# A pooled subtraction streamed through six tile buffers: the last tile subtracted and stored in two halves, the second left to the framework

## The chip, the core and the metric

The kernel runs on one core of one Trainium2 chip. The metric is the device time of one execution in microseconds (us). The profiler also gives the span, from the first to the last instruction, which in these runs is 1.7 to 2.2 us shorter than the time. The record calls an execution slow when it is over 1.5% above the fastest of its kernel.

## The reference

The input is 8 x 4096 x 2112 in fp32. Every four consecutive rows are averaged, and the average is taken from each of the four.

```python
x_r = x.reshape(B, S // stride, stride, D)      # B, S, D = 8, 4096, 2112; stride = 4
pooled = x_r.mean(axis=2)
upsampled = np.repeat(pooled, stride, axis=1)
return (x - upsampled).astype(np.float32)
```

## The kernel before

A group of four rows is one contiguous run of 33,792 bytes. A tile is 128 groups, one per partition, 4224 KB in all; there are n = 64 tiles and six buffers ("slots"). The sync engine (SP) issues the loads, VectorE (DVE) makes three additions and one subtraction per tile, in place (the sums of successive tiles alternate between two buffers, `s_sb` and `s_ps`), and ScalarE (ACT) issues the stores. The section `tile_critical` is synchronised by hand: a load waits for the store that empties its slot, a store for the count of finished subtractions. After it, POOL waits for the last six stores.

```python
def reduce_tile(b, parity):
    rows = slots[b].rearrange("p (f d) -> p f d", f=STRIDE)
    s = s_ps if parity else s_sb
    nc.vector.wait_ge(load_sems[b], 16).then_inc(load_sems[b], -16)
    # ... three additions: s = the sum of the four rows, chained by step_sem
    adds = STRIDE - 1
    nc.vector.wait_ge(step_sem, adds).then_inc(step_sem, -adds)
    nc.vector.scalar_tensor_tensor(
        out=rows, in0=s[:, None, :].to_broadcast([P, STRIDE, D]),
        scalar=-1.0 / STRIDE, in1=rows,
        op0=mybir.AluOpType.mult, op1=mybir.AluOpType.add,
    ).then_inc(done_sem)

with tc.tile_critical():
    for k in range(n):                     # loads, on SP's queue
        # ... b, lap = slot and round of tile k
        load = nc.sync.dma_start(out=slots[b][:], in_=xg[k * P:(k + 1) * P])
        if lap:
            load._wait_ge(store_sems[b], 16 * lap)
        load.then_inc(load_sems[b], 16)
    # ... VectorE: reduce_tile for each tile, in a loop over laps, the rest unrolled
    for k in range(n):                     # stores, on ACT's queue
        # ... b = slot of tile k
        store = nc.scalar.dma_start(out=og[k * P:(k + 1) * P], in_=slots[b][:])
        store._wait_ge(done_sem, k + 1)
        store.then_inc(store_sems[b], 16)
for k in range(n - SLOTS, n):
    total = nc.gpsimd.to_reg(16 * (k // SLOTS + 1))
    tc.keep_in_program_order(nc.gpsimd.wait_ge(store_sems[k % SLOTS], total))
```

## Time and profile before

| | before |
|---|---|
| time, median of the first 3 runs (range) | 1285.41 us (1285.28 to 1285.58) |
| span of the profiled run | 1283.7 us |
| VectorE busy | 1026.4 us, 80% |
| moved | 553.66 MB, mean 431 GB/s |
| last subtraction ends / last store issued / lands | 1268.5 / 1268.6 / 1282.8 us |

The lines behind this table stand in the prediction.

### The profile page before, as it was taken

Reading aid. Unit: us, or ns where it says so; the run is one execution under the profiler, and the core shown is the slowest. Engines: PE = TensorE matmul, PEld = TensorE weight load, DVE = VectorE, ACT = ScalarE, POOL = GpSimd, SP = SyncE. Lnnn points to the kernel's source line nnn. Section 1 sums busy time; section 2 is a strip of 40 time slices with the busy share of each in tenths; the row PEclk is TensorE's granted clock in tenths of the full one; section 3 lists DMA queues with packets and bytes.
Section 4 is the critical chain, followed back from the end, with each engine's and each line's share of the span. In section 5 each row is a group of like instructions: output and inputs, shape, how many; then the busy total and the mean of one; then the engine's idle time right before and its main releaser. Section 6 shows DMA issues by size and latency. Waiting matters only on the chain. (4 is left out here: it accounts for less than half of the span.)

```text
span 1283.7 us, 591 instructions
## 1 busy us (share of the span) xinstructions
DVE 1026.4 (80%) x256; POOL 0.2 (0%) x4
## 2 busy tenths in 40 slices
DVE  5998788787787877878778787787887878878775
POOL 0000000000000000000000000000000000000000
DMA  9999999999999999999999999999999999999999
GB/s 404 421 438 433 426 438 430 431 437 438 430 430 438 431 434 433 438 430 430 438 431 436 431 438 430 430 438 433 435 430 438 430 431 437 438 430 430 438 430 396
DMA packets 18433, 553.66 MB, mean 431 GB/s; under 512 B 2048, under 2 KB 2048, under 8 KB 2048
## 3 DMA queue, kind: packets, MB, share of 16 engines
q1 hardware_dynamic: 9216, 276.83, 50.1%
q10 hardware_dynamic: 9216, 276.83, 50.0%
q14 instruction: 1, 0.01, 0.0%
HBM read 276.82 MB, written 276.82 MB: 431 GB/s over the span
## 5 line engine op out<-in xcount | busy, mean ns | idle before, releaser
L67 DVE SCALAR_TENSOR_TENSOR slot<-s_sb,slot 128x8448 f32<-128x8448 f32 x32 | 286.7, 8958 | 4.7 <-DVEq L66 0.2
L67 DVE SCALAR_TENSOR_TENSOR slot<-s_ps,slot 128x8448 f32<-128x8448 f32 x32 | 286.6, 8957 | 4.7
L59 DVE TENSOR_TENSOR s_sb<-slot 128x2112 f32<-128x2112 f32 x32 | 75.4, 2357 | 120.1 <-DVEq L58 120.1
L59 DVE TENSOR_TENSOR s_ps<-slot 128x2112 f32<-128x2112 f32 x32 | 75.7, 2366 | 108.2 <-DVEq L58 108.2
L62 DVE TENSOR_TENSOR s_ps<-s_ps,slot 128x2112 f32<-128x2112 f32 x64 | 151.4, 2366 | 2.2
L62 DVE TENSOR_TENSOR s_sb<-s_sb,slot 128x2112 f32<-128x2112 f32 x64 | 150.9, 2358 | 2.2
L116 POOL MEMSET const-bfloat16-1.0<- 128x1 bf16 x1 | 0.1, 102 | 0.0
L116 POOL MEMSET const-uint8-127<- 128x1 uint8 x1 | 0.1, 101 | 0.0
L116 POOL MEMSET const-float32-0.0<- 128x1 f32 x1 | 0.1, 99 | 0.2 <-issue 0.2
L116 POOL MEMSET const-float32-1.0<- 128x1 f32 x1 | 0.1, 99 | 0.0
## 6 DMA issues: line engine op xcount, KB each, us to landing
slot<-in_x_dram SPq DMA_DIRECT2D x64, 4224.0 KB, 59.7
out_dram<-slot ACTq DMA_DIRECT2D x64, 4224.0 KB, 43.6
```

What stands on the lines that cost most here:

```text
L59: add = nc.vector.tensor_add(out=s[:], in0=rows[:, 0, :], in1=rows[:, 1, :])
L62: add = nc.vector.tensor_add(out=s[:], in0=s[:], in1=rows[:, f, :])
L67: nc.vector.scalar_tensor_tensor(out=rows, in0=s[:, None, :].to_broadcast([P, STRIDE, D]), scalar=-1.0 / STRIDE, in1=rows, op0=mybir.AluOp ...
L116: nc = _bacc.Bacc("TRN2", target_bir_lowering=False, num_devices=1)
```

## The change

Its intent: start storing the last tile when half of it is subtracted, so that less is left to store after VectorE's last instruction. The second half store stands after the hand-synchronised section, where the framework finds its waits and its semaphore. "By rows" means the rows of a group: the first half is rows 0 and 1 of each group, the first 4224 columns of every partition.

```diff
-    def reduce_tile(b, parity):
+    def reduce_tile(b, parity, cuts=(0, STRIDE)):
...
-        nc.vector.scalar_tensor_tensor(
-            out=rows,
-            in0=s[:, None, :].to_broadcast([P, STRIDE, D]),
...
-        ).then_inc(done_sem)
+        for lo, hi in zip(cuts, cuts[1:]):
+            nc.vector.scalar_tensor_tensor(
+                out=rows[:, lo:hi, :],
+                in0=s[:, None, :].to_broadcast([P, hi - lo, D]),
...
+            ).then_inc(done_sem)
...
+        half = STRIDE // 2
         for b in range(rest):
-            reduce_tile(b, b % 2)
+            reduce_tile(b, b % 2, (0, STRIDE) if b < rest - 1 else (0, half, STRIDE))
...
-            store = nc.scalar.dma_start(out=og[k * P:(k + 1) * P], in_=slots[b][:])
+            cols = W if k < n - 1 else half * D
+            store = nc.scalar.dma_start(
+                out=og[k * P:(k + 1) * P, :cols], in_=slots[b][:, :cols]
+            )
             store._wait_ge(done_sem, k + 1)
             store.then_inc(store_sems[b], 16)
+
+    nc.scalar.dma_start(out=og[G - P:, half * D:], in_=slots[rest - 1][:, half * D:])
```

More of the change, by code (lines that the diff above doesn't have):

```diff
@@ L66, in reduce_tile @@
         nc.vector.wait_ge(step_sem, adds).then_inc(step_sem, -adds)
-        nc.vector.scalar_tensor_tensor(
-            out=rows,
-            in0=s[:, None, :].to_broadcast([P, STRIDE, D]),
-            scalar=-1.0 / STRIDE,
-            in1=rows,
-            op0=mybir.AluOpType.mult,
-            op1=mybir.AluOpType.add,
-        ).then_inc(done_sem)
+        for lo, hi in zip(cuts, cuts[1:]):
+            nc.vector.scalar_tensor_tensor(
+                out=rows[:, lo:hi, :],
+                in0=s[:, None, :].to_broadcast([P, hi - lo, D]),
+                scalar=-1.0 / STRIDE,
+                in1=rows[:, lo:hi, :],
+                op0=mybir.AluOpType.mult,
+                op1=mybir.AluOpType.add,
+            ).then_inc(done_sem)
     assert SLOTS % 2 == 0
```

## The prediction

> **What bounds the kernel now.** I read the first page of the profile from the top: the busy shares, the slices, the transfer queues, and only then the chain that ended last.
>
> ```profile
> DVE 1026.4 (80%) x256; POOL 0.2 (0%) x4
> ...
> DMA  9999999999999999999999999999999999999999
> GB/s 404 421 438 433 426 438 430 431 437 438 430 430 438 431 434 433 438 430 430 438 431 436 431 438 430 430 438 433 435 430 438 430 431 437 438 430 430 438 430 396
> ...
> q1 hardware_dynamic: 9216, 276.83, 50.1%
> q10 hardware_dynamic: 9216, 276.83, 50.0%
> ```
>
> The transfer engines stand at 9 in all forty slices and the load and store queues together fill 100.1% of their time. VectorE (DVE) is at 80%. 64 loads and 64 stores of 4224 KB each are 553.66 MB, and in the middle slices they move at 430 to 438 GB/s. So the kernel is bound by transfers, and the change saves no byte of them. It can only act at the end, and the chain view speaks of VectorE there:
>
> ```profile
> 2 pieces in order of time: start us, us, what
> 1259.48 0.08 issue
> 1259.56 8.96 DVE slot L67
> ```
>
> This is the last tile's subtraction, ending at 1268.5, followed by 15.2 us of the 1283.7 us span in which the view names nothing. That gap is what the change aims at: the last store (4.3 MB) cannot start before the subtraction ends. The question is whether the transfer engines were idle while they waited for it. Two views answer. The first is by stretches (columns: stretch, length, VectorE busy, POOL busy, clock, transfer share, GB/s), from the landing of the last load (the last tile's first add starts at 1252.25) to the issue of the last store, and from there on:
>
> ```profile
> 1252.25:1268.60 16.35, 16.06 (x4) 0.00 (x0) 1.00 1.00 430
> 1268.60:1281.20 12.60, 0.00 (x0) 0.00 (x0) 1.00 0.99 429
> ```
>
> In the first stretch no load is left, the last store is not issued yet, and still the engines are at 1.00 and 430 GB/s. What they move are stores already queued. The second view is the store line, asked in three windows of 20 us, each of which holds the issue of one store, the third last to the last:
>
> ```profile
> L94 ACTq DMA_DIRECT2D out_dram<-slot x1: 338/338/338, 1228.6 to 1228.6; - x1
> DMA to landing us min/median/max: 34.2/34.2/34.2
> ...
> L94 ACTq DMA_DIRECT2D out_dram<-slot x1: 339/339/339, 1248.5 to 1248.5; - x1
> DMA to landing us min/median/max: 24.2/24.2/24.2
> ...
> L94 ACTq DMA_DIRECT2D out_dram<-slot x1: 338/338/338, 1268.6 to 1268.6; - x1
> DMA to landing us min/median/max: 14.2/14.2/14.2
> ```
>
> Issue plus time to landing gives the landings: 1228.6 + 34.2 = 1262.8, 1248.5 + 24.2 = 1272.7, 1268.6 + 14.2 = 1282.8. They lie 9.9 and 10.1 us apart, and one store at 430 to 435 GB/s takes 4.325 MB / 0.43 to 0.435 = 9.9 to 10.1 us. The three stores therefore ran back to back: **the last one was issued 4.1 us before its predecessor landed and stood in line behind it.** VectorE's end isn't what sets the last landing; the queue is. After 1282.8 there remain 0.9 us of semaphores and barriers to 1283.7.
>
> [...]
>
> **The change, part by part.**
>
> (a) The last subtraction in two halves of 4224 columns. [...] First half done at 1259.56 + 4.56 = 1264.1, second at 1268.7.
>
> (b) First half store, 2.163 MB, issued at about 1264.2 in place of 1268.6, 4.4 us earlier. It queues behind the store that lands at 1272.7, as the whole one did. Gain on the time: none. Its share of the line is 5.0 us, so it should land near 1277.7.
>
> (c) Second half store, outside the hand-synchronised section. In the built program it waits until SP has collected the ends of SP, ScalarE's and VectorE's parts of that section, and carries a semaphore of the framework's. Before, SP's collecting step, which stands in the program already, came at 1269.1 with nothing depending on it:
>
> ```profile
> L78 DVEq DRAIN  x1: 8970/8970/8970, 1259.6 to 1259.6; - x1
> L78 ACTq DRAIN  x1: 153/153/153, 1268.9 to 1268.9; - x1
> L78 SPq NOP  x1: 13/13/13, 1269.1 to 1269.1; - x1
> ```
>
> Here VectorE's drain ends at 1268.5, ScalarE drains after issuing the whole store, and SP follows 0.6 us after VectorE. After the change ScalarE has drained long before and VectorE sets the moment: I expect SP at 1268.8 to 1269.1 and the second half issued at 1269.0 to 1269.3, up to 0.7 us **later** than the whole store before. It stands in line behind the first half until about 1277.7. How long does a store take from issue to landing with nothing before it? The first load, 4224 KB with no other in front of it, took 12.4 us (the shortest load in the trace), so about 2.4 us beyond its data. The second half thus needs to be issued only by some 1277.7 - 2.4 = 1275.3; it is there 6 us early. The delay is hidden whole.
>
> (d) Added work of the transfer engines. The bytes are the same; there is one more transfer with its 16 semaphore packets, and 128 rows in two pieces. The pieces per engine are 8 before and 16 after. In the steady state two transfers take 19.97 us (the additions of the even tiles start 1212.31 and 1252.25, four transfers in 39.94), that is 9.985 us each [...]
>
> (e) The end. Before, POOL waits for the store semaphores (its branch comes at 1282.8) and the barrier takes 0.9 us. After, POOL is released at 1277.7 and waits in the barrier; SP waits for the framework's semaphore and joins last. One waiter in place of another: I put it at 0 +- 0.15 us.
>
> Sum: 0 (a, hidden) + 0 (b) + 0 (c) + 0.05 (d) + 0.0 (e). From 1285.41 this gives 1285.46, **1285.5 us**, with the span near 1283.8.
>
> **The rivals.**
>
> The overlap works. If the transfer engines were idle until the last store came, 4.4 us earlier issue of half of it would save up to 4.4 us: 1281.0. For it speaks the chain view, which ends on the subtraction; against it the share of 1.00 and 430 GB/s while the subtraction runs, and the landings 10 us apart. Even this would be 0.3% and inside the 2%.
>
> The framework's store waits for more than the section's ends, such as the landing of the first half. Then it would start at 1277.7 plus about half a microsecond, with some 2.4 us of latency exposed: 1288 us. Against it: its waits in the built program are on the engines' sequencers[...].
>
> The smaller pieces or a shorter tail help. If the engines finish unevenly, half-sized rows could even out the end, or a completion that depends on the last row's size could come up to 0.6 us (half of the 1.25 us in which one engine moves a 33,792-byte row) sooner: 1284.8. Nothing in the trace demands it; the same unevenness may cost as much. The instruction fetch, one packet of 8 KB on the instruction queue, may also fall at another place; a landing shift of a few tenths either way is possible.
>
> **Range and chances.** The three runs before lie within 0.3 us, so the machine's scatter is small; what is uncertain is the tail: 0.15 us in the barrier, up to 0.6 us from the ends of the engines, and a change of session. I take 1284.6 to 1286.2. Faster or slower by 2% would be 25.7 us, more than the whole time after VectorE's last instruction (15.2 us), so neither half store can gain it, and a loss of that size would need a serialisation that no wait in the program makes. Faster 0.005, same 0.985, slower 0.01.
>
> **What would show each step right or wrong.** In the profile after: two subtractions of 128x4224, about 4.56 us each; the first half store issued near 1264.2 and landing near 1277.7, so over 13 us for 5 us of data; the second issued near 1269.2 and landing near 1282.8, over 13 us too; transfer share about 1.0 through to 1281; SP ending a wait near 1282.8 in POOL's place. I am wrong on (b) if the first half lands before 1275, on (c) if the second half is issued after 1271 or the share drops between the halves, on (d) and (e) if the last landing or the barrier moves by over 0.3 us.

The sum came to 0.05 us, all of it from (d), so 1285.41 + 0.05 = 1285.46; that 0.05 is the estimate. It was measured only later (0.050, in the experiment with 256 transfers). For the packets of (d), the pages show 18,433 before and 18,577 after: 144 more, 16 semaphore packets and 128 pieces. The 4.56 us of a half subtraction can be estimated from the trace as well: a straight line through the 2357 ns of an addition of 2112 columns and the 8957 ns of the subtraction of 8448 gives 4557 ns for 4224. And that the waits at the exit of the section don't include landings shows in the kernel before: SP's collecting step came at 1269.1, 13.7 us before the last store landed at 1282.8.

## The result, and the profile after

| | before | after |
|---|---|---|
| time, median of 6 runs (range) | 1285.35 us (1285.09 to 1285.58) | 1285.19 us (1285.04 to 1287.81) |
| ratio of the fast runs | | 1.0002, 95% interval 0.9989 to 1.0015 |
| span of the profiled run | 1283.7 us | 1283.4 us |

The same time. A ratio here is the mean of one kernel's fast runs over the mean of the other's from the same rounds, so it isn't quite the ratio of the medians. One of the six runs after took 1287.81 us and pulls the mean up; without it they lie between 1285.04 and 1285.25. The medians differ by 0.16 us, less than the range of the runs before. Such single runs, 2 to 6 us above the rest, also came with the kernel before (1287.24 us in a later batch) and with an experiment (1291.09 us); what causes them was not looked into.

The chain of waits of the changed kernel (columns: start, length, what) ends with VectorE's drain at the exit of the section, which waits for the second half of the subtraction. It stops at 1268.9, 14.5 us before the end of the span at 1283.4 (15.2 us in the kernel before).

```profile
3 pieces in order of time: start us, us, what
1259.79 0.08 issue
1259.87 4.56 DVE slot L69
1264.43 4.46 DVEq L80
```

The two halves of the subtraction (shortest, median and longest in ns, first and last start):

```profile
L69 DVE SCALAR_TENSOR_TENSOR slot<-s_ps,slot x2: 4545/4551/4557, 1259.9 to 1264.3; 128x4224 f32<-128x4224 f32 x2
```

The same stretches as before, from the landing of the last load to the end of the line (columns as in the prediction), show the transfer engines just as full.

```profile
1252.25:1268.60 16.35, 15.83 (x5) 0.00 (x0) 1.00 1.00 430
1268.60:1281.20 12.60, 0.29 (x1) 0.00 (x0) 1.00 0.99 426
```

The lines of the second last store, of the first half and of the second half (when the transfer was issued, and how long it took to land):

```profile
L98 ACTq DMA_DIRECT2D out_dram<-slot x1: 338/338/338, 1248.9 to 1248.9; - x1
DMA to landing us min/median/max: 23.6/23.6/23.6
...
L98 ACTq DMA_DIRECT2D out_dram<-slot x1: 338/338/338, 1264.5 to 1264.5; - x1
DMA to landing us min/median/max: 13.0/13.0/13.0
...
L104 ACTq DMA_DIRECT2D out_dram<-slot x1: 338/338/338, 1269.1 to 1269.1; - x1
DMA to landing us min/median/max: 13.4/13.4/13.4
```

They land at 1272.5, 1277.5 and 1282.5: back to back again, 5.0 us for each half. The first half was issued 4.1 us earlier than the whole store had been and took 13.0 us for 5.0 us of data. The time it gained at VectorE it spent in line.

The exit of the hand-synchronised section, and the end:

```profile
L80 ACTq DRAIN  x1: 152/152/152, 1264.8 to 1264.8; - x1
L80 SPq NOP  x1: 13/13/13, 1269.0 to 1269.0; - x1
...
L135 POOLq COMPARE_BRANCH  x1: 33/33/33, 1277.5 to 1277.5; - x1
```

ScalarE left the section at 1264.8, VectorE at 1268.9, SP collected both at 1269.0 and the second half went out at 1269.1. POOL came free when the first half landed, at 1277.5 in place of 1282.8; SP waited for the second, and the end came 0.9 us after the last landing, as before.

### The profile page after: what moved, and what is told of

It is laid out like the page before. It is cut to its first block, busy times and chain, and to the rows that moved or that the text cites. A ratio compares the mean times of both kernels' runs of the same rounds, so it can differ in the third digit from the quotient of the medians.

```text
span 1283.4 us, 594 instructions
## 1 busy us (share of the span) xinstructions
DVE 1026.5 (80%) x257; POOL 0.2 (0%) x4
## 2 busy tenths in 40 slices
DMA packets 18577, 553.66 MB, mean 431 GB/s; under 512 B 2064, under 2 KB 2064, under 8 KB 2064
## 5 line engine op out<-in xcount | busy, mean ns | idle before, releaser
L69 DVE SCALAR_TENSOR_TENSOR slot<-s_ps,slot 128x8448 f32<-128x8448 f32 (+1 forms) x33 | 286.7, 8690 | 4.7
```

What stands on the lines that cost most here:

```text
L69: nc.vector.scalar_tensor_tensor(out=rows[:, lo:hi, :], in0=s[:, None, :].to_broadcast([P, hi - lo, D]), scalar=-1.0 / STRIDE, in1=rows[:, ...
```

## The experiments

My theory ("full line"): the stores stand in line at full rate until the end, so an earlier issue of the last one is worth nothing and a somewhat later one costs nothing. The rivals: the split does gain, but the exit of the section gives it back; or the end of the subtraction sets the end after all. Nine kernels were run and all gave the reference's result. They ran on three chips, and each is compared with the runs of the kernel before on its own chip: 1285.27 us for the first four kernels, 1285.29 for the next four and 1285.12 for the last (medians).

### The split without the exit

Both halves are stored inside the section.

```diff
+        last = nc.scalar.dma_start(
+            out=og[G - P:, half * D:], in_=slots[rest - 1][:, half * D:]
+        )
+        last._wait_ge(done_sem, n + 1)
+        last.then_inc(store_sems[rest - 1], 16)      # POOL waits for 16 more
-    nc.scalar.dma_start(out=og[G - P:, half * D:], in_=slots[rest - 1][:, half * D:])
```

> Both halves are stored inside the hand-synchronised section, the second on the count of finished subtractions; no store is left to the framework. Theory (full line): the second half stands behind the first until about 1277.5 whenever it is issued before 1275, so an issue 0.3 to 0.4 us earlier than the 1269.1 of the changed kernel is worth nothing: 1285.2 to 1285.5, within 0.3 us of both kernels. Rival (the exit of the section eats what the split gains): without the exit the split shows its gain, up to 4.4 us, so 1281 to 1284.5.

Measured: 1285.31 us median (1285.12 to 1285.59, and one run of 1291.09) against 1285.27. The second half was issued 0.03 us after VectorE's end (1268.67, issue 1268.70), against 0.17 us in the changed kernel (1268.89, issue 1269.06). So the exit costs 0.14 us on the way to the issue, and taking it away changed nothing in the time. The first rival falls. The lines (start, length), with both stores inside and then in the changed kernel:

```profile
1259.65 9.02 DVE L69 SCALAR_TENSOR_TENSOR slot<-s_ps,slot 128x4224 f32<-128x4224 f32 x2
1268.70 0.34 ACTq L103 DMA_DIRECT2D out_dram<-slot  x1
```
```profile
1259.87 9.02 DVE L69 SCALAR_TENSOR_TENSOR slot<-s_ps,slot 128x4224 f32<-128x4224 f32 x2
1269.06 0.34 ACTq L104 DMA_DIRECT2D out_dram<-slot  x1
```

### A late last tile: whole and in halves

If the line hides the issue of the last store, there must be a delay that it hides and one that it doesn't. Additions that nothing uses are put ahead of the last subtraction, 2 (4.8 us) or 4 (9.5 us), in the kernel before and in the changed one.

```diff
+        for j in range(extra):          # extra = 2 or 4 on the last tile, else 0
+            add = nc.vector.tensor_add(out=s_sb[:], in0=rows[:, 2, :], in1=rows[:, 3, :])
+            add._wait_ge(step_sem, STRIDE - 1 + j)
+            add.then_inc(step_sem)
-        adds = STRIDE - 1
+        adds = STRIDE - 1 + extra
```

> The kernel before, with two idle-purpose additions (2.4 us each) ahead of the last tile's subtraction: the whole last store is issued about 4.8 us later, near 1273.4. Theory (full line): an unhindered store lands some 12.4 us after its issue, so it lands near 1285.8 and 1.8 us of the 4.8 are absorbed: +3.0 us (2.6 to 3.6), 1288.4. Rival (the subtraction's end sets the end): +4.8 us, 1290.2.

> The changed kernel with the same two additions ahead of the last tile's subtraction. Theory (full line): the first half is issued near 1269.3, still behind the line that ends at 1272.5, and the second near 1273.9, before the 1275 at which it would be needed: 0 us (-0.3 to +0.3), so about 3 us faster than the whole store with the same delay. Rival (the subtraction's end sets the end, the change only redistributes): +4.8 us, like the whole store.

> The kernel before with four such additions, 9.6 us: the last store is issued near 1278.2. Theory (full line): 1.8 us absorbed, lands near 1290.6, +7.8 us (7.3 to 8.4), 1293.2; transfer share falls visibly between 1272 and 1279. Rival: +9.6 us, 1295.0.

> The changed kernel with four additions (9.6 us) ahead of the last subtraction. Theory (full line): first half issued near 1274.1, nothing before it, lands near 1281.5; second issued near 1278.7, lands near 1286.5: +4.0 us (3.3 to 4.6), 1289.2, about 4 us faster than the whole store with the same delay. Rival (the subtraction's end sets the end): +9.6 us, like the whole store.

| | time, us | against before on the same chip |
|---|---|---|
| whole, 2 additions | 1287.42 (1287.24 to 1287.65) | +2.15 |
| halves, 2 additions | 1285.23 (1285.10 to 1285.33) | -0.04 |
| whole, 4 additions | 1292.63 (1292.19 to 1293.77) | +7.36 |
| halves, 4 additions | 1288.00 (1287.72 to 1288.18) | +2.71 |

The second rival, which wanted the full delay each time, falls. The split saves 2.2 us where the whole store is 4.9 us late and 4.6 us where it is 9.9 us late. It saves nothing at no delay, because there is nothing exposed to save. The store line of the whole store with 2 additions, and the transfer share at the time the line runs out, with 2 and with 4 additions and then in the kernel before:

```profile
L98 ACTq DMA_DIRECT2D out_dram<-slot x1: 338/338/338, 1273.5 to 1273.5; - x1
DMA to landing us min/median/max: 11.3/11.3/11.3
...
1271.00:1275.00 4.00, 2.44 (x1) 0.00 (x0) 1.00 0.31 135
```
```profile
1271.00:1275.00 4.00, 4.00 (x1) 0.00 (x0) 1.00 0.00 0
```
```profile
1271.00:1275.00 4.00, 0.00 (x0) 0.00 (x0) 1.00 1.06 456
```

The share falls to 0.31 and to 0.00: these transfer engines do wait for VectorE, which they did not do at the end of the kernel before (1.06 in the same window; a share can exceed 1, as a packet is counted whole where it starts). And the lines give a number that the prediction lacked: with nothing ahead of it a whole store lands 11.3 us after its issue (11.4 with 4 additions), not 12.4, and a half one 6.4 us after it (the first half with 4 additions). So in the kernel before, where the whole store took 14.2 us, it stood 2.9 us in line, and in the changed kernel the second half, which took 13.4 us, stood 7.0 us in line. The four kernels' sizes follow within 0.4 us: the whole store 4.9 and 9.9 us late should cost +2.0 and +7.0, measured +2.15 and +7.36; the second half 4.5 and 9.4 us late 0 and +2.4, measured -0.04 and +2.71. Of the expectations, the one for halves with 2 additions was met. The other three came out 0.4 to 1.3 us too high, two of them outside their ranges (whole with 2 additions and halves with 4), since they took 12.4 us for the unhindered store; their signs and order held.

### Only the second half late

The four additions stand between the two half subtractions of the changed kernel.

```diff
         for lo, hi in zip(cuts, cuts[1:]):
+            if lo:
+                for j in range(4):
+                    add = nc.vector.tensor_add(out=s_sb[:], in0=rows[:, 2, :], in1=rows[:, 3, :])
+                    ...                              # chained by step_sem, waited for
```

> The changed kernel with the four additions (9.6 us) between the two half subtractions, so only the second half store is late, issued near 1278.7. Theory (full line): it was needed only by about 1275 and lands 7.4 us after its issue, near 1286.1: +3.6 us (2.9 to 4.2), 1288.9; 6 us of the delay are absorbed. Rival (the second half store sets the end directly): +9.6 us, 1294.8.

Measured: 1287.83 us (1287.40 to 1288.10), +2.54. The second half was issued at 1278.94 in place of 1269.06 and landed 6.4 us later.

```profile
L111 ACTq DMA_DIRECT2D out_dram<-slot x1: 338/338/338, 1278.9 to 1278.9; - x1
DMA to landing us min/median/max: 6.4/6.4/6.4
```

Of 9.9 us of delay, 7.3 us were absorbed. That fits the profile of the changed kernel, where the half took 13.4 us to land instead of 6.4: 7.0 us in line. This is the slack of the store left to the framework, against the 0.14 us that the exit of the section costs it. The expectation of +3.6 us (2.9 to 4.2) was missed for the same reason as above: it had 6 us of slack.

### A shorter line

Four slots in place of six, in both kernels. Fewer tiles are under way, so fewer stores can stand in line (the second last store lands 18.7 us after its issue in place of 24.2): with the whole store the last load lands later (the last tile's additions start at 1258.8 in place of 1252.3), and more of the stores have been moved by then. The last four tiles are unrolled, as the split needs them.

```diff
-SLOTS = 6
+SLOTS = 4
-    laps, rest = divmod(n, SLOTS)
+    laps, rest = n // SLOTS - 1, SLOTS
```

> The kernel before with four tile buffers in place of six: fewer stores can stand in line. A buffer's round is then about 80 us (load, 16 us of additions and subtraction, store) instead of 120, so a store should land some 24 us after issue instead of 44 and at most one store stands before the last one. Theory (full line): the line runs dry before the last subtraction ends; the last store lands about 12.4 us after issue and the time is 2 to 8 us longer than with six buffers. Rival (the length of the line does not matter): within 1 us of six buffers.

> The changed kernel with four tile buffers. Theory (full line): with the line dry the split saves what the chain of waits promised: 2 to 4.5 us faster than the whole last store with four buffers. Rival (the split never helps, because the exit of the section or the smaller pieces cost as much): within 1 us of it.

Measured: whole 1290.41 us (1289.53 to 1290.47), +5.12; halves 1287.53 us (1286.37 to 1287.74), +2.24. The split saves 2.9 us. The stretch from 1272 to 1282 and the last store of the whole kernel, then of the halves (there the landing line holds both halves, 8.0 and 8.4 us):

```profile
1272.00:1282.00 10.00, 3.10 (x1) 0.00 (x0) 1.00 0.65 280
...
L95 ACTq DMA_DIRECT2D out_dram<-slot x1: 338/338/338, 1275.1 to 1275.1; - x1
DMA to landing us min/median/max: 11.3/11.3/11.3
```
```profile
1272.00:1282.00 10.00, 3.88 (x1) 0.00 (x0) 1.00 1.01 431
...
DMA to landing us min/median/max: 8.0/8.2/8.4
```

With the whole store the line ran dry (share 0.65) and the store took the unhindered 11.3 us. With halves the first one, issued at 1271.5, kept the line full (1.01). So no delay made by hand is needed for the split to pay; it is enough that the line is short. Both kernels are slower than with six slots, so this is no improvement on either. What the halves lose against six slots lies near the start: from 20 to 80 us the engines move 421, 431 and 411 GB/s in stretches of 20 us, against 431, 434 and 433, which is 1.6 us of transfers, and the last landing is 1.6 us later (1284.4 against 1282.8).

### The price of one more transfer

Every load and store of the kernel before is cut into two column halves: 256 transfers in place of 128.

```diff
-            load = nc.sync.dma_start(out=slots[b][:], in_=xg[k * P:(k + 1) * P])
+            for c in (0, W // 2):
+                load = nc.sync.dma_start(
+                    out=slots[b][:, c:c + W // 2], in_=xg[k * P:(k + 1) * P, c:c + W // 2]
+                )
...                                  # the stores likewise; waits for 32 in place of 16
```

> The kernel before with every load and every store cut into two transfers of 2112 KB, 256 in place of 128, the subtractions whole. It measures the price of one more transfer, which the prediction put at 0.05 us. Theory (a small fixed cost per transfer and per piece): 128 more transfers x 0.044 us (the gap in the packet records between the whole and the split last store) = +5.6 us (4.5 to 7), 1290.9. Rival (extra transfers cost nothing while the line is full): within 0.5 us.

Measured: 1291.51 us (1291.25 to 1291.68) against 1285.12, +6.39, or 0.050 us per added transfer. The cost is spread evenly: the additions of a tile half way start 2.72 us later than before (616.08 against 613.36), those of the last tile 5.66 us later (1257.91 against 1252.25). The changed kernel pays it once, and its own traces show that. A trace also keeps the start and duration of every packet (the packet records), and each transfer ends with 16 semaphore packets (2048 packets under 512 B for the 128 transfers of the kernel before). The semaphore packets of the last whole store come on average 9.98 us after those of the store before it, those of the second half in the changed kernel 10.03 us after those of that store (10.03 also with both halves inside the section). Whether it belongs to the transfer or to its pieces was not separated, as this cut doubles both.

Of the nine expectations six were met, and three fell short by the same mis-sized term. No experiment points to a version that beats both kernels. By the packet records of the kernel before, all 16 engines are busy from 2.5 us after the start to 1281.0, 2.7 us before the end, and the last packet ends at 1282.3. What remains is bytes and the price per transfer.

## Why the prediction was right

The median of 1285.19 us lies in the range of 1284.6 to 1286.2, 0.3 us below the predicted 1285.5, and "same" within 2% was given 0.985. The total alone tests little, since any sum of terms within a few tenths of a microsecond would have fitted it. The terms are tested by the traces and the experiments.

- **The bound.** Right. The landings 10 us apart and the share of 1.00 in the kernel before showed it; late last tiles and four slots showed that the gain appears as soon as the share falls, and only then.
- **(a)** Right: 4.545 and 4.557 us against 4.56 predicted. The second starts just before the first ends, so that the two together take 9.02 us, 0.06 us more than the whole (8.96).
- **(b)** Right: issued at 1264.5 (predicted 1264.2; VectorE ran 0.3 us later in this execution, before the change acts), landed at 1277.5 (1277.7), gain none.
- **(c)** Right in its mechanism, mis-sized in one term. The issue at 1269.1 was predicted within 1269.0 to 1269.3. But an unhindered store needs 1.4 us beyond its data, not 2.4: 11.3 us less 9.9 for a whole one and 6.4 less 5.0 for a half. I had taken 2.4 from the first load. By the packet records, 0.85 us of the difference lies between its first packet and the end of its data (11.0 us, against 10.15 for the last store with 2 additions): its first 16 packets took 1.4 to 2.1 us each, all later ones about 1.25. Loads waiting behind it did not slow those later packets; whether the first ones were slow because five more loads were being issued then (until 3.9 us), because it is a load, or because the program starts, was not tried. The slack is therefore 7.0 us, not 6.
- **(d)** Right: the 0.05 us predicted was the author's estimate; 0.050 was measured with 128 more (6.39 us), and 10.03 in place of 9.98 us in the packet records of the change itself. In the time of the changed kernel it can't be seen: the last landing came 0.3 us earlier, not 0.05 later, at the edge of what the prediction allowed. That difference is not the change's. On average the 16 semaphore packets of the last store came at the same time in both (1281.48 and 1281.49). The last of them came 0.84 us after this average before and 0.58 us after, and the lag was the same already in the whole store ahead.
- **(e)** Right: SP in place of POOL, 0.9 us from the last landing to the end in both.
- **The rivals.** "The overlap works" failed with six slots, and held in part with four: 2.9 us of the 4.4. "The framework waits for the landing of the first half" failed: the second half was issued 8.4 us before it. A slightly shorter tail can't be told from scatter: the last landing came 0.3 us earlier in the one profiled run, but the split inside the section, with the same pieces, came out at 1285.31 us against 1285.27. By the packet records the last store's semaphore packets lie 0.85 us apart, as those of the whole store ahead of it do, so the smaller pieces did not even out the end. In the kernel before, a store's 16 semaphore packets came 0.4 to 0.6 us apart and 1.2 us in its last three stores, and 0.14 us where the line had run dry first (the whole store after two more additions). What sets the distance was not tried.

Where did the expected gain go, then? It was never on the path that sets the end. What the change did buy is slack: the last store may now be 7 us late instead of 2.9 before the time moves.

## What to carry to other kernels

Before splitting a last tile, don't look at when its compute ends but at how long its store takes to land against a store with nothing ahead of it: here 14.2 us against 11.3, so it stood in line, and issuing it earlier only lengthened the wait. The chain of waits names the last instruction with a late end; it doesn't say that the transfer after it was waiting for that instruction. The same split paid 2.2 to 4.6 us here where the line was short, from fewer buffers or a slower last tile, so it is a matter of the line and not of the split.
